# Per-chunk offsets on another engine, one gate moved, one branch begun with a gate, and rows split by two engines

## The chip, the cores and the metric

The kernel runs on one core of a Trainium2 chip. The core has five engines that work side by side, each through its own queue in order: TensorE (PE, matmuls), VectorE (DVE), ScalarE (ACT), GpSimd (POOL) and SyncE (SP, here the issuer of all DMAs). PEld in the profile is TensorE's loading of weights. The metric is the device time of one execution in microseconds; less is better.

## The reference

Two layers of a decoder, 1024 tokens of width 1024, 16 learned meta tokens in front (1040 rows), fp32. Cut to what matters:

```python
def hybrid_layer(x, ...):
    h = rmsnorm(x, norm_g)
    proj = h @ w_in                       # split into A, B, C and the gates
    log_f = log_sigmoid(a_f + b_f)        # 8 heads
    log_cum = cumsum(log_f, axis=1)
    y_a = forgetting attention(a_q, a_k, a_v, log_cum)
    cq, ckv = rmsnorm(b_cq, g_cq), rmsnorm(b_ckv, g_ckv)
    y_b = latent attention(cq @ w_uq, ckv @ w_ukv, rotary key b_kr)
    y_c = sliding-window attention with sinks(rope(c_q), rope(c_k), c_v)
    # y_n * silu(z_n) @ w_branch[n], n = 0, 1, 2, merged by sigmoid gates
    m = sum(sigmoid(gates[n]) * ((y_n * silu(z_n)) @ w_branch[n]))
    return x + m @ w_out
```

## The kernel before

All activations lie transposed: channels on the 128 partitions, rows (tokens) on the free axis, cut into chunks `FULL` (264, 264, 512 columns), `TOK` (two of 512) in layer 2 where only the tokens count, and `END` (four of 256) for the rows of the output projection. Every fp32 product is three matmuls on a high and a low part of each operand, `mm3` (L175 hh with wh, L176 hl with wh, L177 hh with wl). `split` makes the two parts: the high part is a cast on ACT (L157), the low part a subtraction (L158), on DVE for activations and on POOL for weights (`weights`, L158 `wl<-wr,wh`). Results land in PSUM banks named `ps_s`, `ps_pj`, `ps_t`, `ps_o`, two of each; a bank is used again when the engine that empties it is through.

A layer goes through these stages:

- **Side work and sliding-window projections.** `side_work` is a generator that computes the cumulative log-forget values on 8 partitions, beside the projections of C's keys and queries (`rotate`, L222 to L232, on DVE and POOL; casts of `sg`, L157, on ACT; L227 and L230 read the banks). The cumulative sum is made in nine cuts (16 and eight of 128 columns): a scan per cut (L579), the last column of each into `tot` (L581), a scan over the nine totals into `off` (L585), and the addition of each offset to its cut (L587).
- **Low rank, values, kn and wuq.** The latent rows are projected and normed (`normed`, L201 to L212, on DVE with two ACT steps), then come `values` (L454 to L461: value blocks of 256 columns, emptied by DVE L459 and ACT L461 in turn), the keys `kn` in four pairs (casts and subtractions of `sg`, L157 and L158) and the queries `wuq`. Between these, `some()` is called at ten positions, and `EARLY[l]` says how many gate projections are run at each: positions 0 to 2 lie among the values, 3 to 6 after the four kn pairs, 7 to 9 after the parts of wuq. A gate projection is two or three chunks of 24 matmuls each, emptied by ACT alone (L657, `gt`) and written to memory.
- **Fox, mla, swa.** The three attentions. Between their blocks `fill()` takes the next entry of a list, `PLAN[l]`: `g` is a gate projection, `z` the projection of a SiLU path (ACT `ez` L734, then DVE `zs` L735 empties the bank), `r` and `s` belong to the merge. The first `fill()` of each attention stands ahead of its first block.
- **Merge.** `branch(n_, d)` for n_ = 0, 2, 1 and d = 0 to 7: per chunk the gate through a tanh (ACT L951), 12 matmuls into a bank, DVE L957 (`gt<-gt,ps`) and, for n_ of 2 and 1, DVE L958 (`acc<-acc,gt`). For n_ = 1, the last, the sum is split into `m` for the output projection, in chunks `och` of 264, 264 and 512 (layer 1) or four of 256 (layer 2).
- **Output projection (wo)**, from `m`, column by column, and in layer 2 the final norm.

Tile builds the program and orders the instructions of each engine by its own simulated timeline, so the order on an engine isn't the order of the code, and an edit can move instructions that it doesn't name. All DMAs stand in SP's queue.

Of the kernel before, what the change touches and what calls it, by code (L numbers as in the profile page):

```python
# [13 lines left out]
AF = mybir.ActivationFunctionType  # L14
ALU = mybir.AluOpType
# [3 lines left out]
P = 128  # L19
# [3 lines left out]
NM = 16  # L23
# [30 lines left out]


EARLY = ((1, 0, 0, 0, 0, 0, 0, 1, 0, 0),
         (0, 0, 0, 0, 1, 0, 0, 0, 0, 0))

# [10 lines left out]
def _f(ap):  # L71
    return ap.bitcast(F32)
# [13 lines left out]
def tile_kernel(ctx: ExitStack, tc, a, out):  # L86
    nc = tc.nc
# [66 lines left out]
    def split(hi, lo, src, scale=None, eng=None):  # L154

        if scale is None:
            nc.scalar.copy(hi, src)  # L157
            (eng or nc.vector).tensor_tensor(lo, src, _f(hi), ALU.subtract)  # L158
        else:
            nc.scalar.activation(hi, src, AF.Copy, scale=scale)  # L160
            nc.vector.scalar_tensor_tensor(lo, src, scale, _f(hi), ALU.mult, ALU.subtract)

    def weights(src, n):
        raw = wp.tile([P, 1024], F32, tag="wr", name="wr", bufs=2)
        dma(raw[:, :n], src)
        wh = wp.tile([P, 1024], F32R, tag="wh", name="wh")
        wl = wp.tile([P, 1024], F32R, tag="wl", name="wl")
        split(wh[:, :n], wl[:, :n], raw[:, :n], eng=nc.gpsimd)
        return wh, wl

    def mm3(dst, wh, wl, rh, rl, nk, m, c0, c1):

        for k in range(nk):
            w1 = wh[:, k * P:k * P + m]
            nc.tensor.matmul(dst, w1, rh[:, k, c0:c1], start=(k == 0), stop=False)  # L175
            nc.tensor.matmul(dst, w1, rl[:, k, c0:c1], start=False, stop=False)  # L176
            nc.tensor.matmul(dst, wl[:, k * P:k * P + m], rh[:, k, c0:c1],  # L177
                             start=False, stop=(k == nk - 1))
# [343 lines left out]
    for l in range(DEPTH):  # L522
# [33 lines left out]
        def side_work():  # L556

            c16 = pa.tile([32, L], F32, tag="c16", name="c16", bufs=1)
            s16 = pa.tile([64, L], F32, tag="s16", name="s16", bufs=1)
            dma(c16, a["c16"][:32])  # L560
            dma(s16[32:64], a["sn16"])
            fr = pa.tile([H, L], F32, tag="fr", name="fr", bufs=1)
            x = pa.tile([H, L], F32, tag="fx", name="fx", bufs=1)
            e = pa.tile([H, L], F32, tag="fe", name="fe", bufs=1)
            nc.scalar.copy(fr, krt[64:72])
            nc.vector.tensor_scalar(x, fr, bfc[:, l:l + 1], None, ALU.add)
            nc.vector.scalar_tensor_tensor(e, x, -1.0, x, ALU.mult, ALU.min)
            nc.scalar.activation(e, e, AF.Exp)
            nc.scalar.activation(e, e, AF.Ln, bias=ones[:H, 0:1])
            yield  # L570
            nc.vector.scalar_tensor_tensor(x, x, 0.0, e, ALU.min, ALU.subtract)
            cuts = [(0, NM)] + [(NM + i * P, NM + (i + 1) * P) for i in range(NB)]
            z8 = pa.tile([H, P], F32, tag="z8", name="z8", bufs=1)
            nc.vector.memset(z8, 0.0)
            tot = pa.tile([H, 16], F32, tag="tot", name="tot", bufs=1)
            off = pa.tile([H, 16], F32, tag="off", name="off", bufs=1)
            nc.vector.memset(off, 0.0)
            for n_, (c0, c1) in enumerate(cuts):
                nc.vector.tensor_tensor_scan(e[:, c0:c1], x[:, c0:c1], z8[:, :c1 - c0], 0.0,  # L579
                                             ALU.add, ALU.add)  # L580
                nc.vector.tensor_copy(tot[:, n_:n_ + 1], e[:, c1 - 1:c1])  # L581
                if n_ == 4:
                    yield
            yield
            nc.vector.tensor_tensor_scan(off[:, 1:10], tot[:, 0:9], z8[:, :9], 0.0, ALU.add, ALU.add)  # L585
            for n_, (c0, c1) in enumerate(cuts):
                nc.vector.tensor_scalar(e[:, c0:c1], e[:, c0:c1], off[:, n_:n_ + 1], None, ALU.add)  # L587
            dma(ck_d, e)
            yield
            r1 = pa.tile([32, L], F32, tag="r1", name="r1", bufs=1)  # L590
            r2 = pa.tile([32, L], F32, tag="r2", name="r2", bufs=1)
            kr = [pa.tile([32, L], F32R, tag=f"kr{x_}", name="kr", bufs=1) for x_ in range(2)]
            nc.vector.tensor_tensor(r1, krt[0:32], c16, ALU.mult)
            nc.vector.tensor_tensor(r2, krt[32:64], s16[32:64], ALU.mult)
            yield
            nc.vector.tensor_tensor(r1, r1, r2, ALU.add)
            split(kr[0], kr[1], r1)
            for n_ in range(2):
                dma(kr_d[n_], kr[n_])
# [129 lines left out]
        def filler(br):  # L729
            plan, zs = list(PLAN[l][(0, 2, 1)[br]]), []  # L730

            def ev_z(t, c0, c1):
                e = fin.tile([P, 512], F32, tag="gt", name="ez", bufs=GT)[:, :c1 - c0]
                nc.scalar.activation(e, t, AF.Tanh, scale=0.5)  # L734
                nc.vector.scalar_tensor_tensor(zs[-1][:, c0:c1], e, 1.0, t, ALU.add, ALU.mult)  # L735

            def fill():
                for kind in plan.pop(0) if plan else "":
                    if kind == "r":
                        merge_starts()  # L740
                    elif kind == "s":
                        branch(0, merged.pop(0), "pj")
                    elif kind == "z":
                        zs.append(fin.tile([P, L], F32, tag="zs", name="zs", bufs=2))
                        proj(w1[T_Z + 4 * br + len(zs) - 1], KD, hh, hl, qch, ev_z, tag="pj")
                    elif kind == "g":
                        gate(fin, "pj")
                finish_late()
            return fill, zs
# [72 lines left out]
        with tc.tile_pool(name=f"swk{l}", bufs=2, side=A, reuse_waits="tile") as pk, \  # L822
# [12 lines left out]
            for kv in range(2):  # L835
# [14 lines left out]
                for i in range(-1 if first else 0, NB):  # L850
# [90 lines left out]
        def branch(n_, d, tag=None):  # L941

            if d % 2 == 0:
                wbr[:] = weights(a["wbr"][l, n_, d // 2], 1024)
            w = [x[:, 512 * (d % 2):512 * (d % 2) + 512] for x in wbr]
            gr = (gp2 if gp2 and d % 2 else gp).tile([P, L], F32, tag="gt", name="gt", bufs=2)
            dma(gr[:, lo:], gate_d[KD * n_ + d, :, lo:])
            for c0, c1 in qch:
                n = c1 - c0
                g = gr[:, c0:c1]  # L950
                nc.scalar.activation(g, g, AF.Tanh, scale=0.5)  # L951
                t = (psum(tag) if tag else dense())[:, :n]
                mm3(t, w[0], w[1], ys[0], ys[1], 4, P, c0, c1)
                if n_ == 0:
                    nc.vector.scalar_tensor_tensor(acc[:, d, c0:c1], g, 1.0, t, ALU.add, ALU.mult)
                else:
                    nc.vector.scalar_tensor_tensor(g, g, 1.0, t, ALU.add, ALU.mult)  # L957
                    nc.vector.tensor_tensor(acc[:, d, c0:c1], acc[:, d, c0:c1], g, ALU.add)  # L958
            if n_ == 1:
                for c0, c1 in och:  # L960
                    split(mt[c0][0][:, d], mt[c0][1][:, d], acc[:, d, c0:c1])

        with tc.tile_pool(name=f"mla{l}", bufs=2, side=B, reuse_waits="tile") as pm:
            fill, zs = filler(1)
# [68 lines left out]
        with tc.tile_pool(name=f"so{l}", bufs=2, side=B, reuse_waits="tile") as po:  # L1033
# [21 lines left out]
            for c0, c1 in och:  # L1055
# [6 lines left out]
                else:  # L1062
# [110 lines left out]
```

## Time and profile before

| | |
|---|---|
| median of 3 runs | 2587.16 us (2586.63 to 2590.52) |
| profiled execution, its own time | 2592.05 us |
| its span, first to last instruction | 2590.3 us |
| mean granted TensorE clock | 0.993 |
| TensorE busy | 98% of the span |
| DVE, ACT, POOL busy | 50%, 46%, 38% |
| DMA | 303.40 MB, mean 117 GB/s |

The page says for each engine how long it worked; since TensorE works nearly all the time, the page's averages say little about this change. What is to be read are the few places at which TensorE stands: the windows (busy time by stretch, with the granted clock), the table of waits (which instruction released the waiting one), and the rows of single instructions in order of time, in which a bracket `[idle before <-releaser]` stands behind an instruction that had to wait. In a row, `64x512` are partitions and elements per partition, and `x3` three instructions of one group drawn together.

### The profile page before, as it was taken

The numbers are of one execution on the slowest core, as the hardware profiler recorded it, in microseconds if no ns is written. First come the engines' busy times: TensorE is split into PE (matmuls) and PEld (weight loads), VectorE is DVE, ScalarE is ACT, GpSimd is POOL, SyncE is SP. The second block draws the span as 40 slices with busy tenths as digits, with TensorE's granted clock in tenths as the row PEclk, the third lists the DMA queues.
The fourth block names the chain that finished last, engine by engine and source line by source line (L and its number), as shares of the span: only waits on it lengthen the run. The fifth ranks groups of instructions, "written<-read, shape, count | busy, mean of one in ns | idle before, by whom it ended". The sixth has DMA issues, their size and how long they took to land.

```text
span 2590.3 us, 42110 instructions
## 1 busy us (share of the span) xinstructions
PE 2527.6 (98%) x15446; PEld 2256.7 (87%) x15446; DVE 1286.9 (50%) x3339; ACT 1199.9 (46%) x2684; POOL 996.0 (38%) x966
## 2 busy tenths in 40 slices
PE   8999999999999999999999999999999999999998
PEld 7989899999888999899998878888887888887887
DVE  6464355544363445657156453455434623565743
ACT  5234345545474456644232333455445634666433
POOL 2141545354332424462523325445323332353433
PEclk9999999999999999999999999999999999999999
DMA  5144512222634434364333353221226363453532
GB/s 169 55 136 136 205 54 81 73 74 79 172 104 118 124 98 127 101 225 167 112 90 87 105 197 128 74 80 60 90 71 177 101 167 84 124 140 129 173 123 74
DMA packets 137631, 303.40 MB, mean 117 GB/s; under 512 B 22560, under 2 KB 63296, under 8 KB 137424
## 3 DMA queue, kind: packets, MB, share of 16 engines
q1 hardware_dynamic: 137424, 300.71, 37.7%
q8 instruction: 122, 2.00, 0.3%
q14 instruction: 85, 0.70, 0.1%
HBM read 211.98 MB, written 88.66 MB: 116 GB/s over the span
## 4 chain that ended last, share of the span: by engine, by line
PE 77%; DMA 5%; DVE 4%; ACT 2%; issue 2%; POOL 1%; SPq 1%; POOLq 0%; ACTq 0%; DVEq 0%
PE ps_pj L175 14%; PE ps_pj L176 14%; PE ps_pj L177 14%; PE ps_t L268 5%; PE ps_s L999 3%; PE ps_o L312 3%; PE ps_o L310 2%; PE ps_s L176 2%; PE ps_s L175 2%; PE ps_s L177 2%; PE ps_s L804 1%; PE ps_s L802 1%; PE ps_o L176 1%; PE ps_o L175 1%; PE ps_o L177 1%
## 5 line engine op out<-in xcount | busy, mean ns | idle before, releaser
L158 POOL TENSOR_TENSOR wl<-wr,wh 128x1024 fp32r<-128x1024 f32 (+1 forms) x156 | 376.6, 2414 | 838.3 <-ACT wh L157 712.2
L175 PE MATMUL ps_pj<-hh,wh 128*128 128x512 f32 (+1 forms) x1920 | 674.3, 351 | 3.6 <-DVE zs L735 2.2
L176 PE MATMUL ps_pj<-hl,wh 128*128 128x512 f32 (+1 forms) x1920 | 672.7, 350 | 0.0
L177 PE MATMUL ps_pj<-hh,wl 128*128 128x512 f32 (+1 forms) x1920 | 671.3, 350 | 1.4 <-POOL wl L158 1.4
L175 PEld LDWEIGHTS ps_pj<-hh,wh 128*128 128x128 f32 x1920 | 363.2, 189 | 46.6 <-DVE zs L735 3.2
L177 PEld LDWEIGHTS ps_pj<-hh,wl 128*128 128x128 f32 x1920 | 363.4, 189 | 43.0 <-POOL wl L158 2.0
L176 PEld LDWEIGHTS ps_pj<-hl,wh 128*128 128x128 f32 x1920 | 363.1, 189 | 39.8 <-issue 0.5
L158 DVE TENSOR_TENSOR ptl<-ps_t,pth 128x512 fp32r<-128x512 f32 (+1 forms) x386 | 244.7, 641 | 140.6 <-ACT pth L157 134.3
L157 ACT CAST pth<-ps_t 128x512 fp32r<-128x512 f32 (+1 forms) x386 | 205.8, 547 | 169.0 <-PE ps_t L268 140.9
L260 ACT ACTIVATE P<-P,mn 128x656 f32<-128x656 f32 (+8 forms) x272 | 206.9, 761 | 164.7 <-DVE mn L255 160.1
L157 ACT CAST wh<-wr 128x1024 fp32r<-128x1024 f32 (+1 forms) x156 | 162.1, 1039 | 249.9 <-PE ps_pj L176 146.9
L268 PE MATMUL ps_t<-ident,P 128*128 128x128 f32 x1152 | 187.6, 276 | 0.8 <-DVE ptl L158 0.7
L310 PE MATMUL ps_o<-pth,vp 128*128 128x256 f32 (+1 forms) x640 | 168.4, 278 | 4.5 <-DVE u L281 3.1
L312 PE MATMUL ps_o<-ptl,vp 128*128 128x256 f32 (+1 forms) x640 | 160.4, 288 | 2.4 <-DVE ptl L158 2.2
L298 POOL COPY pmeta<-P 128x16 f32<-128x16 f32 x256 | 49.6, 198 | 276.2 <-ACT P L260 272.8
L999 PE MATMUL ps_s<-kt,qt 96*128 96x328 f32 (+9 forms) x696 | 146.8, 328 | 3.1 <-DVE mn L255 3.0
L268 PEld LDWEIGHTS ps_t<-ident,P 128*128 128x128 f32 x1152 | 134.9, 141 | 9.0 <-DVE ptl L158 1.5
L310 PEld LDWEIGHTS ps_o<-pth,vp 128*128 128x128 f32 x640 | 121.4, 190 | 13.2 <-issue 3.0
L809 POOL TENSOR_TENSOR cm<-ckb,tri 128x128 f32<-128x128 f32 (+1 forms) x136 | 60.4, 446 | 184.9 <-DVE mn L255 181.4
L312 PEld LDWEIGHTS ps_o<-ptl,vp 128*128 128x128 f32 x640 | 121.2, 189 | 9.2 <-DVE ptl L158 5.4
L281 DVE TENSOR_TENSOR u<-ps_o,hv 64x256 f32<-64x256 f32 x128 | 53.9, 421 | 138.0 <-ACT hv L280 121.6
L999 PEld LDWEIGHTS ps_s<-kt,qt 96*128 96x128 f32 (+1 forms) x696 | 108.5, 187 | 10.3 <-DVE mn L255 5.5
(353 smaller groups left out, 5645.8 us busy)
## 6 DMA issues: line engine op xcount, KB each, us to landing
wr<-in_w_dram SPq DMA_DIRECT2D x108, 512.0 KB
gate_d<-gt SPq DMA_DIRECT2D x72, 256.0 KB
gt<-gate_d SPq DMA_DIRECT2D x24, 520.0 KB
wr<-in_wbr_dram SPq DMA_DIRECT2D x24, 512.0 KB
gt<-gate_d SPq DMA_DIRECT2D x24, 512.0 KB
kn_d<-sg SPq DMA_DIRECT2D x16, 520.0 KB
ckb<-ck_d SPq DMA_DIRECT2D x16, 520.0 KB
kt<-kn_d SPq DMA_DIRECT2D x16, 520.0 KB
```

The lines of the kernel that those rows point to most:

```text
L157: nc.scalar.copy(hi, src)
L158: (eng or nc.vector).tensor_tensor(lo, src, _f(hi), ALU.subtract)
L175: nc.tensor.matmul(dst, w1, rh[:, k, c0:c1], start=(k == 0), stop=False)
L176: nc.tensor.matmul(dst, w1, rl[:, k, c0:c1], start=False, stop=False)
L177: nc.tensor.matmul(dst, wl[:, k * P:k * P + m], rh[:, k, c0:c1], start=False, stop=(k == nk - 1))
L260: nc.scalar.activation(s[:rows, :n], s[:rows, :n], AF.Exp, bias=prev, scale=-1.0, accum_out=total)
L268: nc.tensor.transpose(t[:kk, c:c + rows], src, ident[:rows, :rows])
L281: nc.vector.tensor_tensor(u[mine, :n], o[mine, :n], t[mine, :n], ALU.add)
L310: nc.tensor.matmul(dst, vp[:, j + x, vs], ph[:, cols], start=(j + x == 0), stop=False)
L312: nc.tensor.matmul(dst, vp[:, j + x, vs], pl[:, cols], start=False, stop=(diag and x == 1))
L809: nc.gpsimd.tensor_tensor(cm[:rows, :rows], ckb[:rows, d:n], tri[:rows, :rows], ALU.add)
L999: nc.tensor.matmul(dst, q[:, qi, q0:q0 + rows], kt[:, ki, c0:c1], start=(x == 0), stop=(x == 2))
```

## The change

Four edits:

1. In `side_work`, both layers: the nine copies into `tot` become one ACT copy of a strided column set, and the nine additions of the offsets (L587) become ACT activations of the kind Identity with the offset as bias.
2. `EARLY[1]`: layer 2's one early gate is taken from position 4 (after the second kn pair) to position 1 (among the values).
3. `PLAN[1][0]`, fox of layer 2: the first fill is a gate; the first z comes a fill later, and a later fill runs one gate fewer, so that nine gates and four z remain.
4. In `branch` with n_ = 1: the rows are split as soon as their chunk of `acc` is summed, no longer after all chunks of d, and of the pieces in `och` those with an odd number have their low part subtracted on POOL. In layer 1 this is the second of three (8 subtractions of 264 columns), in layer 2 the second and fourth of four (16 of 256).

```diff
--- before.py
+++ after.py
@@ -54,7 +54,7 @@
 
 
 EARLY = ((1, 0, 0, 0, 0, 0, 0, 1, 0, 0),
-         (0, 0, 0, 0, 1, 0, 0, 0, 0, 0))
+         (0, 1, 0, 0, 0, 0, 0, 0, 0, 0))
 
 
 
@@ -62,7 +62,7 @@
     ("z . z . . . gg g . g z g z g g . gg".split(),
      "gg zzg . . . gg zz . gg".split(),
      "g g . z g z g . g g zzr s . . sss s s".split()),
-    ("z . . . z . gg . . gg z . z g gg . gg".split(),
+    ("g z . . z . g . . gg z . z g gg . gg".split(),
      "gg zg z g . gg zz g gg".split(),
      "g gg . z . z g . . g zzr . ss . ss s s".split()),
 )
@@ -578,13 +578,13 @@
             for n_, (c0, c1) in enumerate(cuts):
                 nc.vector.tensor_tensor_scan(e[:, c0:c1], x[:, c0:c1], z8[:, :c1 - c0], 0.0,
                                              ALU.add, ALU.add)
-                nc.vector.tensor_copy(tot[:, n_:n_ + 1], e[:, c1 - 1:c1])
                 if n_ == 4:
                     yield
+            nc.scalar.copy(tot[:, :9], e[:, NM - 1::P])
             yield
             nc.vector.tensor_tensor_scan(off[:, 1:10], tot[:, 0:9], z8[:, :9], 0.0, ALU.add, ALU.add)
             for n_, (c0, c1) in enumerate(cuts):
-                nc.vector.tensor_scalar(e[:, c0:c1], e[:, c0:c1], off[:, n_:n_ + 1], None, ALU.add)
+                nc.scalar.activation(e[:, c0:c1], e[:, c0:c1], AF.Identity, bias=off[:, n_:n_ + 1])
             dma(ck_d, e)
             yield
             r1 = pa.tile([32, L], F32, tag="r1", name="r1", bufs=1)
@@ -956,9 +956,11 @@
                 else:
                     nc.vector.scalar_tensor_tensor(g, g, 1.0, t, ALU.add, ALU.mult)
                     nc.vector.tensor_tensor(acc[:, d, c0:c1], acc[:, d, c0:c1], g, ALU.add)
-            if n_ == 1:
-                for c0, c1 in och:
-                    split(mt[c0][0][:, d], mt[c0][1][:, d], acc[:, d, c0:c1])
+                if n_ == 1:
+                    for i, (m0, m1) in enumerate(och):
+                        if c0 <= m0 < c1:
+                            split(mt[m0][0][:, d], mt[m0][1][:, d], acc[:, d, m0:m1],
+                                  eng=nc.gpsimd if i % 2 else None)
 
         with tc.tile_pool(name=f"mla{l}", bufs=2, side=B, reuse_waits="tile") as pm:
             fill, zs = filler(1)
```

No matmul and no DMA is added or taken away. In layer 1 the order of TensorE's instructions is the same in both kernels; in layer 2 it differs in the values, kn, wuq and fox.

First place, DVE in layer 1's side work (`fe` are the cumulative sums, `ro` and `sg` the rotated rows of C's projections and their split). Before:

```order
L228 TENSOR_TENSOR ro_1100<-cx_1097,s_977 64x512
L227 TENSOR_TENSOR ro_1099<-ps_t,c_976 64x512
L230 TENSOR_TENSOR ro_1102<-ps_t,s_977 64x512
L585 SCALAR_TENSOR_TENSOR off<-tot,z_1278 8x9
L158 TENSOR_TENSOR sg_983<-ro_1060,sg_982 64x264
L587 TENSOR_SCALAR fe<-fe,off 8x128 x5
L229 TENSOR_TENSOR ro_1101<-cx_1097,c_976 64x512
L587 TENSOR_SCALAR fe<-fe,off 8x128 x3
L228 TENSOR_TENSOR ro_1188<-ps_s,s_977 128x264
L158 TENSOR_TENSOR sg_981<-ro_1099,sg_980 64x512
L227 TENSOR_TENSOR ro_1187<-ps_o,c_976 128x264
L230 TENSOR_TENSOR ro_1190<-ps_o,s_977 128x264
```

and after:

```order
L158 TENSOR_TENSOR sg_981<-ro_1058,sg_980 64x264
L227 TENSOR_TENSOR ro_1099<-ps_t,c_976 64x512
L228 TENSOR_TENSOR ro_1100<-cx_1097,s_977 64x512
L585 SCALAR_TENSOR_TENSOR off<-tot,z_1278 8x9
L230 TENSOR_TENSOR ro_1102<-ps_t,s_977 64x512
L158 TENSOR_TENSOR sg_983<-ro_1060,sg_982 64x264
L229 TENSOR_TENSOR ro_1101<-cx_1097,c_976 64x512
L228 TENSOR_TENSOR ro_1188<-ps_s,s_977 128x264
L158 TENSOR_TENSOR sg_981<-ro_1099,sg_980 64x512
L432 MEMSET xm 128x96
L227 TENSOR_TENSOR ro_1187<-ps_o,c_976 128x264
L230 TENSOR_TENSOR ro_1190<-ps_o,s_977 128x264
```

The additions into `fe` are gone from between the rotation's steps; the scan into `off` moved ahead of L230 of the 512-column chunk, and `ps_o` is read by L227 and L230 behind the subtraction into `sg` as before. On ACT, in the same place, the offsets now stand between the casts; after:

```order
L157 CAST sg_980<-ro_1058 64x264
L614 COPY cx_1097<-ps_t 64x512
L583 COPY tot<-fe 8x9
L587 ACTIVATE fe<-fe,off 8x16
L157 CAST sg_982<-ro_1060 64x264
L587 ACTIVATE fe<-fe,off 8x128 x8
L157 CAST sg_980<-ro_1099 64x512
L157 CAST wh<-wr 128x1024
L157 CAST sg_982<-ro_1101 64x512
```

Second place, ACT in layer 2 from the last value blocks to the kn pairs (`cqh` is the high part of the normed cq, `vst` value blocks, `gt` the early gate, `sg` kn). Before:

```order
L461 COPY vst<-ps_s 128x256 x3
L157 CAST cqh<-ps_o 128x512
L447 COPY vst<-ps_s 16x256
L447 COPY vst<-ps_pj 16x256
L157 CAST cqh<-ps_o 128x512 x3
L157 CAST sg_16853<-ps_s 128x264
L157 CAST sg_16853<-ps_pj 128x264
L157 CAST sg_16853<-ps_s 128x512
L157 CAST sg_16884<-ps_pj 128x264
L157 CAST sg_16884<-ps_s 128x264
L157 CAST sg_16884<-ps_pj 128x512
L657 COPY gt<-ps_s 128x512
```

and after:

```order
L157 CAST cqh<-ps_o 128x512
L461 COPY vst<-ps_s 128x256
L157 CAST cqh<-ps_o 128x512 x2
L657 COPY gt<-ps_s 128x512
L157 CAST cqh<-ps_o 128x512 x3
L157 CAST wh<-wr 128x768
L657 COPY gt<-ps_pj 128x512
L461 COPY vst<-ps_s 128x256 x3
L447 COPY vst<-ps_s 16x256
L447 COPY vst<-ps_pj 16x256
L157 CAST sg_16899<-ps_s 128x264
L157 CAST sg_16899<-ps_pj 128x264
```

The gate's two copies (`gt`) moved from behind the second kn pair (six casts into `sg`) to between the value blocks, ahead of the last three `vst` and of all kn pairs.

Third place, DVE at the end of n_ = 1 in layer 2 (`gt<-gt,ps` and `acc` as above, `m` the low parts). Before:

```order
L957 SCALAR_TENSOR_TENSOR gt<-gt,ps_pj 128x512
L958 TENSOR_TENSOR acc<-acc,gt 128x512
L158 TENSOR_TENSOR m_26272<-acc,m_26271 128x256
L158 TENSOR_TENSOR m_26274<-acc,m_26273 128x256
L957 SCALAR_TENSOR_TENSOR gt<-gt,ps_t 128x512
L958 TENSOR_TENSOR acc<-acc,gt 128x512
L158 TENSOR_TENSOR m_26268<-acc,m_26267 128x256
L957 SCALAR_TENSOR_TENSOR gt<-gt,ps_o 128x512
L158 TENSOR_TENSOR m_26270<-acc,m_26269 128x256
L958 TENSOR_TENSOR acc<-acc,gt 128x512
L158 TENSOR_TENSOR m_26272<-acc,m_26271 128x256
L158 TENSOR_TENSOR m_26274<-acc,m_26273 128x256
```

and after:

```order
L957 SCALAR_TENSOR_TENSOR gt<-gt,ps_s 128x512
L958 TENSOR_TENSOR acc<-acc,gt 128x512
L158 TENSOR_TENSOR m_26252<-acc,m_26251 128x256
L957 SCALAR_TENSOR_TENSOR gt<-gt,ps_pj 128x512
L958 TENSOR_TENSOR acc<-acc,gt 128x512
L158 TENSOR_TENSOR m_26256<-acc,m_26255 128x256
L957 SCALAR_TENSOR_TENSOR gt<-gt,ps_t 128x512
L958 TENSOR_TENSOR acc<-acc,gt 128x512
L158 TENSOR_TENSOR m_26252<-acc,m_26251 128x256
L957 SCALAR_TENSOR_TENSOR gt<-gt,ps_o 128x512
L958 TENSOR_TENSOR acc<-acc,gt 128x512
L158 TENSOR_TENSOR m_26256<-acc,m_26255 128x256
```

On POOL, in the same stretch, the other half of the subtractions stands between the low parts of the weights; after:

```order
L158 TENSOR_TENSOR wl<-wr,wh 128x1024
L158 TENSOR_TENSOR m_26258<-acc,m_26257 128x256
L158 TENSOR_TENSOR m_26254<-acc,m_26253 128x256
L158 TENSOR_TENSOR m_26258<-acc,m_26257 128x256
L158 TENSOR_TENSOR m_26254<-acc,m_26253 128x256
L158 TENSOR_TENSOR wl<-wr,wh 128x1024
L158 TENSOR_TENSOR m_26258<-acc,m_26257 128x256
L158 TENSOR_TENSOR wl<-wr,wh 128x1024
```

Of the two subtractions of a chunk, one is left on DVE, always behind its `acc`.

## The prediction

> **What bounds the kernel now.** I read the page's first part, then windows of the stages that the change touches, then TensorE's waits, and at each wait the rows of the engines in order of time.
>
> ```profile
> span 2590.3 us, 42110 instructions
> PE 2527.6 (98%) x15446; PEld 2256.7 (87%) x15446; DVE 1286.9 (50%) x3339; ACT 1199.9 (46%) x2684; POOL 996.0 (38%) x966
> ```
>
> TensorE (PE) is busy for 2527.6 of 2590.3 us and loses no instruction by the change. So only its 62.7 us without work, and stretches in which its clock is halved, can give time back; the other engines' busy shares don't matter by themselves. A window row gives its length, the busy time and count of PE, PEld, DVE, ACT and POOL, then the granted clock (PEclk), DMA share and GB/s:
>
> ```profile
> 120.00:140.00 20.00, 15.46 (x82) 13.87 (x81) 19.45 (x42) 6.43 (x11) 11.99 (x10) 0.83 0.35 82
> 1380.00:1400.00 20.00, 20.00 (x87) 16.16 (x86) 19.30 (x41) 7.14 (x11) 8.14 (x6) 1.00 0.18 59
> 1400.00:1420.00 20.00, 18.61 (x81) 14.77 (x80) 17.36 (x25) 6.39 (x10) 14.16 (x10) 1.00 0.42 108
> 1480.00:1500.00 20.00, 19.11 (x118) 16.25 (x116) 10.33 (x17) 8.48 (x17) 2.55 (x2) 1.00 0.30 93
> 1500.00:1520.00 20.00, 16.95 (x89) 14.16 (x88) 11.76 (x23) 6.03 (x14) 0.00 (x0) 0.91 0.57 214
> 1560.00:1580.00 20.00, 17.83 (x94) 15.56 (x93) 3.01 (x6) 3.52 (x7) 12.04 (x10) 0.91 0.67 233
> 2480.00:2500.00 20.00, 16.20 (x121) 15.96 (x121) 9.12 (x16) 6.63 (x14) 6.05 (x3) 0.91 0.59 226
> ```
>
> The row 1380 to 1400 shows PE undisturbed: 87 matmuls in 20 us, 0.23 us each. The other rows are stages of the change, with 4.54, 1.39, 0.89, 3.05, 2.17 and 3.80 us in which PE stood. A clock of 0.91 means that another 0.09 x 20 = 1.8 us of clock are lost there, and 0.83 means 3.4 us, part of it while PE stood anyway. The clock falls in the windows with waits of 2.2 us and more, and not in the one with 1.39 us. The waits and what released them (total, times, longest):
>
> ```profile
> PE ps_o L175 <- DVE ro L230: 4.5, 1, 4.5
> PE ps_s L175 <- ACT m L157: 3.7, 1, 3.7
> PE ps_s L175 <- DVE sg L158: 2.4, 1, 2.4
> PE ps_pj L175 <- DVE zs L735: 2.2, 1, 2.2
> ```
>
> **A and B: the offsets go to ScalarE.** Layer 1's side work:
>
> ```profile
> 123.29 0.94 DVE L585 TENSOR_TENSOR_SCAN off<-tot,z 8x9 f32<-8x9 f32 x1
> 124.23 0.62 ACT L157 CAST sg<-ro 64x512 fp32r<-64x512 f32 x1 [2.71 <-POOL ro L231]
> 124.49 1.06 DVE L587 TENSOR_SCALAR fe<-fe,off 8x128 f32<-8x128 f32 x5
> 126.08 4.08 DVE L587 TENSOR_SCALAR fe<-fe,off 8x128 f32<-8x128 f32 x3
> 126.29 1.28 POOL L232 TENSOR_TENSOR ro<-ro,ro 64x512 f32<-64x512 f32 x1 [2.09 <-DVE ro L229]
> 127.54 2.34 POOL L158 TENSOR_TENSOR wl<-wr,wh 128x1024 fp32r<-128x1024 f32 x1
> 131.48 0.42 DVE L230 TENSOR_TENSOR ro<-ps_o,s 128x264 f32<-128x264 f32 x1
> 131.96 0.59 PE L175 MATMUL ps_o<-hh,wh 128*128 128x264 f32 x1 [4.54 <-DVE ro L230]
> L333 ACT ACTIVATE rt<-ps_t 18x128 f32<-18x128 f32 x8 | 2.1, 265 | 8.5 <-PE ps_t L331 8.5
> ```
>
> Five additions (L587) take 1.06 us, and the last three take 4.08 us: they end only after GpSimd's (POOL's) two instructions have ended at 129.88. Behind them on VectorE (DVE) stands L230, which frees the bank that PE waits for. The change takes all nine additions and the nine copies ahead of the scan off VectorE. ScalarE (ACT) gets one copy and nine activations, ahead of its cast of sg. No row shows such an activation. The 18x128 row bounds it from above at 0.27 us; from below I take the 0.20 us between VectorE's starts (1.06 us for five). Eight cost 1.6 to 2.1 us. In the new order the scan stands before one of the three 512-column steps that it stood behind, and without the copies it starts about 1.2 us earlier and ends at 123.0; the activations end at about 125, the cast at 125.7. VectorE's subtraction behind the cast may be held by L232 until about 126.3 and ends at 127.0; L227 and L230 follow by 127.7. PE wants the bank at 131.96 - 4.54 = 127.4, so 0.3 us of wait are left, and the halved clock behind it goes. Of its 3.4 us some 1.2 fall on idle time: 2.2 count. The most is 4.5 + 2.2 = 6.7; the least 3.0, if a wait of 1.5 us stays; I take 5.5, near the upper end since the additions are gone from the queue. ScalarE's casts of weights come half a microsecond later, which costs nothing: PE has the rest of the group of two chunks to work off before it uses them.
>
> [...]
>
> B: in layer 2 the same additions stall the same way, and PE's 1.39 us in the window 1400 to 1420 lie ten microseconds behind that, for weights that GpSimd makes late. VectorE comes 3.7 us earlier to them. Bounds 0 (the weights are late anyway) and 1.4; I take 1.2.
>
> **C: the early gate among the values (layer 2).**
>
> ```profile
> 1508.06 0.73 DVE L212 SCALAR_TENSOR_TENSOR ps_o<-raw,gcol,ps_t 128x512 f32<-128x512 f32 x1
> 1510.06 0.42 DVE L158 TENSOR_TENSOR sg<-ps_s,sg 128x264 fp32r<-128x264 f32 x1
> 1510.54 0.39 PE L175 MATMUL ps_s<-cvh,wh 128*128 128x264 f32 x1 [2.38 <-DVE sg L158]
> 1527.10 0.43 DVE L158 TENSOR_TENSOR sg<-ps_s,sg 128x264 fp32r<-128x264 f32 x1 [12.18 <-ACT sg L157]
> ```
>
> VectorE is late with the norm of cq (L212) and the copies of values, so PE waits up to 2.38 us for banks; a few microseconds on, VectorE is idle for 12.18 us, since the gate that PE then works on needs only ScalarE. The gate is 48 matmuls, 48 x 0.23 = 11.0 us. It now stands after ten value blocks, so VectorE works off its arrears under it. The 0.89 us before 1500 stay, as they lie ahead of it; the 3.05 us and 1.8 us of clock behind can go: at most 4.85, at least 2 if a new wait of 2 us comes elsewhere. I take 4.3. What is late next: the kn pairs now follow each other without the gate's 11 us between, but the casts and subtractions of one pair (six of each) fit under its matmuls, as they do at 1527; and the 768-column weights, which start once the gate has left its buffer, are needed behind eighteen value matmuls.
>
> **D: the forgetting branch begins with a gate (layer 2).**
>
> ```profile
> 1567.39 1.04 ACT L157 CAST wh<-wr 128x1024 fp32r<-128x1024 f32 x1 [8.32 <-PE ps_pj L176]
> 1568.34 1.08 ACT L734 ACTIVATE ez<-ps_pj 128x512 f32<-128x512 f32 x2
> 1568.96 1.29 DVE L735 SCALAR_TENSOR_TENSOR zs<-ez,ps_pj 128x512 f32<-128x512 f32 x2 [10.47 <-ACT ez L734]
> 1569.70 0.39 PE L175 MATMUL ps_pj<-hh,wh 128*128 128x264 f32 x1 [2.17 <-DVE zs L735]
> ```
>
> ScalarE's cast of weights, its first ez and VectorE's zs stand in a chain before the bank is free. With a gate, one copy (L657) takes the place of ez and zs. The bank is free 0.65 us earlier (1569.65 less the end of the first ez at about 1569.0), and the wait becomes 1.5 us, about the length at which no halved clock was seen. Least 0.6, most 2.17 + 1.8 = 4.0; I take 2.2, as the cast stays in front. The later exchange of a z fill for a gate in that stage leaves PE's work equal; I put it at 0, within 1 either way, since no row here prices it.
>
> **E: merged rows split chunk by chunk (n = 1, layer 2).**
>
> ```profile
> 2470.03 0.68 DVE L957 SCALAR_TENSOR_TENSOR gt<-gt,ps_t 128x512 f32<-128x512 f32 x1
> 2472.47 0.68 DVE L957 SCALAR_TENSOR_TENSOR gt<-gt,ps_o 128x512 f32<-128x512 f32 x1
> 2473.43 2.92 POOL L158 TENSOR_TENSOR wl<-wr,wh 128x1024 fp32r<-128x1024 f32 x1 [7.90 <-ACT wh L157]
> 2474.56 2.07 DVE L158 TENSOR_TENSOR m<-acc,m 128x256 fp32r<-128x256 f32 x1 [0.47 <-ACT m L157]
> 2476.55 0.68 DVE L957 SCALAR_TENSOR_TENSOR gt<-gt,ps_s 128x512 f32<-128x512 f32 x1
> 2481.87 0.68 DVE L957 SCALAR_TENSOR_TENSOR gt<-gt,ps_t 128x512 f32<-128x512 f32 x1
> 2484.09 0.68 DVE L957 SCALAR_TENSOR_TENSOR gt<-gt,ps_o 128x512 f32<-128x512 f32 x1
> L958 DVE TENSOR_TENSOR acc<-acc,gt 128x512 f32<-128x512 f32 x48 | 47.0, 986 | 0.9
> L222 POOL TENSOR_TENSOR sq<-sq,sqt 128x256 f32<-128x256 f32 x24 | 17.5, 739 | 31.4 <-ACT sqt L221 31.4
> ```
>
> A chunk of this branch is 12 matmuls, 12 x 0.23 = 2.8 us. VectorE needs 2.44 us (2470.03 to 2472.47), and 4.08 where a subtraction sits under GpSimd's wl; three plain chunks and one such make 11.4 against PE's 11.1, so it never catches up and PE waits 3.7 us (the waits above) for the last rows. After: one of two subtractions per chunk is GpSimd's, and VectorE's chunk is 2.2 us, as from 2481.87 to 2484.09, which holds one of them. Over 16 chunks this gives 16 x 0.24 = 3.8 us, and where the delayed one is now GpSimd's, 1.6 more for each. GpSimd's 16 subtractions cost 0.74 each by the nearest form (L222), 3.0 in four chunks beside 2.9 of wl: it has time. The window's 3.80 + 1.8 us are the most; the least is below nothing (rivals); I take 4.3. Layer 1's same branch (1160 to 1240) has PE busy throughout, so it gives 0:
>
> ```profile
> 1160.00:1240.00 80.00, 80.00 (x511) 72.87 (x510) 53.42 (x90) 30.95 (x60) 24.94 (x13) 1.00 0.49 165
> ```
>
> [...]
>
> **Sum.** 5.5 + 1.2 + 4.3 + 2.2 + 4.3 = 17.5 us. The profiled execution took 2592.05 us, 4.9 above the median of the runs, 2587.16; less 17.5 it is 2574.5, and on the runs' scale 2569.7. I say 2570.
>
> **Rivals.**
> First: GpSimd's subtractions hold VectorE. A held one costs at most its 0.74 us, the 2.07 row shows that holding happens. If it hits one addition into acc per chunk, VectorE's chunk is 2.9 us against 2.8, no arrears are made up, E gives 0: 2574. For it: VectorE's acc step has two operands in SBUF like the held m. Against: GpSimd's step falls mostly beside gt, which reads PSUM.
> Second, on the other side: the same holding, but of both VectorE steps of a chunk (acc and m), and of GpSimd's own wl. VectorE's chunk is then 2.2 + 1.5 = 3.7 us, 0.9 over PE's; 16 x 0.9 = 14 us are added at the end of the branch, with PE at half clock for perhaps half of it (7). E is then -21, and the sum -21 + 13.2 = -8: 2595, slower. It decides when VectorE's chunk passes 3.3 us: 16 x 0.5 x 1.5 = 12 eats the rest.
> Third: ScalarE, now in the chain, is late by 2 us or more, since its activations wait for the scan and the cast for them: A gives 3, B 0, 2573.5; with D's halved clock staying as well, 2575.5.
> Fourth: the halved stretches merely move to other waits, and new waits for VectorE appear behind the kn pairs; A, C, D and E keep a third: 2581 to 2585, about no change.
>
> **How the numbers follow.** Forecast, four or five of the waits gone: 0.58. First rival 0.15, third 0.10, fourth 0.11 (half of it within 0.2%), second 0.06. 0.2% is 5.2 us, about what can be told from no change here. Faster by over 0.2%: 0.58 + 0.15 + 0.10 + 0.05 = 0.88, less 0.03 from the forecast's own tail: 0.85; within: 0.09; slower: 0.06. Range: the upper ends 6.7 + 1.4 + 4.85 + 2.4 + 5.6 = 21 give 2566, and with up to 4 more for D's cast and smaller waits 2562; at the other end the three partial rivals reach 2576, and half of the fourth 2583.
>
> **What would show it.** A: no L587 on DVE, the wait for ro L230 under 1 us, clock 1.00 in 120 to 140. B: no wait for wl near 1413. C: the 12-us idle of DVE gone, the wait for sg L158 gone. D: the wait for zs at the start of fox replaced by one of about 1.5 us for ACT's gt. E: the wait for m at the start of wo under 1 us, while the mean of L958 128x512 (986 ns in the groups above) stays. Wrong would be: a longer L958, a wait of PE for ACT sg in the side work, or halved clocks at other places.

## The result: 14 us less, and the profile after

| | before | after |
|---|---|---|
| median | 2587.63 us (6 runs, 2586.63 to 2590.52) | 2574.41 us (6 runs, 2569.85 to 2578.36) |
| ratio | | 0.9946, 95% interval 0.9933 to 0.9959 |
| profiled execution | 2592.05 us | 2569.85 us |
| span, mean granted clock | 2590.3 us, 0.993 | 2567.8 us, 0.998 |

The ratio is 14.0 us (10.6 to 17.3); the medians differ by 13.2. The two profiled executions are 22.2 us apart: the one of before took longer than its six timed runs, and the one of after is the fastest of its six. So the traces tell where time went, and the timed runs how much. Two of e1's twelve executions below took 8764 and 9988 us and are left out of its ratio. The stages of the change after it, as windows (columns as in the prediction):

```profile
120.00:140.00 20.00, 18.99 (x127) 17.28 (x126) 17.20 (x26) 9.12 (x22) 15.58 (x12) 1.00 0.50 134
1380.00:1400.00 20.00, 18.58 (x80) 14.75 (x79) 18.61 (x33) 8.68 (x20) 10.40 (x8) 1.00 0.35 87
1480.00:1500.00 20.00, 19.73 (x115) 16.91 (x115) 16.62 (x27) 9.32 (x19) 2.16 (x2) 1.00 0.49 153
1500.00:1520.00 20.00, 20.00 (x126) 17.97 (x125) 7.30 (x16) 7.33 (x17) 1.15 (x2) 1.00 0.61 227
1540.00:1560.00 20.00, 18.05 (x100) 15.10 (x99) 2.40 (x6) 6.45 (x10) 12.17 (x9) 1.00 0.98 356
2460.00:2480.00 20.00, 19.55 (x161) 19.15 (x161) 7.89 (x14) 7.49 (x16) 8.96 (x7) 1.00 0.63 246
```

TensorE stands 1.01, 1.42, 0.27, 0, 1.95 and 0.45 us there, where it stood 4.54, 1.39, 0.89, 3.05, 2.17 and 3.80, and the clock is 1.00 in all six. What is left of the waits:

```profile
PE ps_pj L175 <- ACT gt L657: 2.0, 2, 1.4
PE ps_s L177 <- POOL wl L158: 1.4, 1, 1.4
PE ps_pj L177 <- POOL wl L158: 0.9, 1, 0.9
PE ps_s L175 <- ACT m L157: 0.4, 1, 0.4
```

Layer 1's side work (prediction's A) in order of time:

```profile
121.58 2.45 ACT L587 ACTIVATE fe<-fe,off 8x128 f32<-8x128 f32 x8 [0.44 <-DVE off L585]
124.57 1.30 DVE L158 TENSOR_TENSOR sg<-ro,sg 64x512 fp32r<-64x512 f32 x1 [0.33 <-ACT sg L157]
126.26 0.42 DVE L230 TENSOR_TENSOR ro<-ps_o,s 128x264 f32<-128x264 f32 x1
125.57 2.55 POOL L158 TENSOR_TENSOR wl<-wr,wh 128x1024 fp32r<-128x1024 f32 x1 [0.24 <-ACT wh L157]
128.17 0.39 PE L177 MATMUL ps_pj<-hh,wl 128*128 128x264 f32 x1 [0.93 <-POOL wl L158]
```

L230 is through at 126.7, so the bank is no longer what PE waits for. It waits 0.93 us for the weights' low part (wl), which GpSimd starts only at 125.57. Of that, 0.24 us is GpSimd's wait for ScalarE's cast, which stands behind the eight activations (2.45 us from the first to the last); ahead of it GpSimd ran L232 from 124.05 to 125.33. In layer 2 (B) the longest wait for wl is as long as before, but it is another one. First before's, from the table of waits, then the rows of after:

```profile
PE ps_pj L177 <- POOL wl L158: 1.4, 1, 1.4
1393.04 1.04 ACT L157 CAST wh<-wr 128x1024 fp32r<-128x1024 f32 x1
1394.64 1.30 POOL L231 TENSOR_TENSOR ro<-ro,ro 128x512 f32<-128x512 f32 x1 [2.17 <-DVE ro L227]
1395.90 2.37 POOL L158 TENSOR_TENSOR wl<-wr,wh 128x1024 fp32r<-128x1024 f32 x1
1398.32 0.50 PE L177 MATMUL ps_s<-hh,wl 128*128 128x512 f32 x1 [1.42 <-POOL wl L158]
```

Before waited in `ps_pj` (at 1415). After doesn't wait there; it waits in `ps_s`, some 30 matmuls earlier in the program, where before didn't. The cast for this wl was done at 1394.08, but in GpSimd's new order wl stands behind L231 (in before it stood ahead of it), and L231 waited 2.17 us for VectorE's L227.

In the place of D, ScalarE's cast of weights still stands ahead of the copy:

```profile
1551.76 1.04 ACT L157 CAST wh<-wr 128x1024 fp32r<-128x1024 f32 x1 [7.52 <-PE ps_pj L176]
1552.71 1.07 ACT L657 COPY gt<-ps_pj 128x512 f32<-128x512 f32 x2
1553.35 0.40 PE L175 MATMUL ps_pj<-hh,wh 128*128 128x264 f32 x1 [1.39 <-ACT gt L657]
```

### The profile page after: what moved, and what is told of

Same layout as the page of the kernel before. It is cut to its first block, busy times and chain, and to the rows that moved or that the text cites. A ratio compares the mean times of both kernels' runs of the same rounds, so it can differ in the third digit from the quotient of the medians.

```text
span 2567.8 us, 42092 instructions
## 1 busy us (share of the span) xinstructions
PE 2517.1 (98%) x15446; PEld 2247.5 (88%) x15446; DVE 1273.4 (50%) x3279; ACT 1205.8 (47%) x2704; POOL 1012.9 (39%) x990
## 4 chain that ended last, share of the span: by engine, by line
PE 79%; DMA 5%; DVE 2%; ACT 2%; POOL 2%; issue 1%; SPq 0%; POOLq 0%; ACTq 0%; DVEq 0%
PE ps_pj L175 14%; PE ps_pj L176 14%; PE ps_pj L177 14%; PE ps_t L268 5%; PE ps_s L1001 3%; PE ps_o L312 3%; PE ps_o L310 2%; PE ps_s L177 2%; PE ps_s L176 2%; PE ps_s L175 2%; PE ps_s L804 1%; PE ps_s L802 1%; PE ps_o L176 1%; PE ps_o L177 1%; PE ps_o L175 1%
## 5 line engine op out<-in xcount | busy, mean ns | idle before, releaser
L176 PEld LDWEIGHTS ps_pj<-hl,wh 128*128 128x128 f32 x1920 | 361.4, 188 | 39.4 <-issue 0.5
```

## The experiments

Times are ratios to the kernel before, timed beside it on the same chip, and the same in us of 2588. The last five columns are TensorE's waits in that kernel's one trace: A and B in the two side works, C before the kn pairs, D at fox's start in layer 2, E at the start of layer 2's output projection.

| kernel | ratio (interval) | us | A | B | C | D | E |
|---|---|---|---|---|---|---|---|
| before | 1 | | 4.5 | 1.4 | 2.4 | 2.2 | 3.7 |
| after | 0.9946 (0.9933 to 0.9959) | -14.0 | 0.9 | 1.4 | 0 | 1.4 | 0.4 |
| e1 offsets alone | 0.9974 (0.9963 to 0.9986) | -6.7 | 0.9 | 1.4 | 2.4 | 2.2 | 3.4 |
| e2 early gate alone | 0.9967 (0.9954 to 0.9980) | -8.5 | 4.5 | 1.4 | 0 | 2.1 | 1.6 |
| e3 fox's plan alone | 0.9979 (0.9969 to 0.9989) | -5.4 | 4.5 | 1.4 | 2.4 | 1.4 | 2.3 |
| e4 split alone | 0.9996 (0.9987 to 1.0004) | -1.0 | 4.5 | 1.4 | 2.4 | 2.2 | 0.3 |
| e5 after again | 0.9948 (0.9931 to 0.9965) | -13.5 | 0.9 | 1.4 | 0 | 1.4 | 0 |
| e6 after without the split | 0.9962 (0.9947 to 0.9977) | -9.8 | 0.9 | 1.4 | 0 | 1.4 | 3.6 |
| e7 after, split on VectorE alone | 0.9956 (0.9943 to 0.9969) | -11.4 | 0.9 | 1.4 | 0 | 1.4 | 0 |
| e8 after, gate a position later | 0.9944 (0.9927 to 0.9960) | -14.5 | 0.9 | 1.4 | 0 | 1.4 | 0.3 |
| e9 copies of totals alone | 0.9982 (0.9970 to 0.9994) | -4.7 | 2.0 | 0.4 | 2.4 | 2.2 | 1.7 |
| e10 after, one addition on VectorE | 0.9967 (0.9955 to 0.9978) | -8.5 | 3.4 | 2.1 | 0 | 1.4 | 0.8 |
| e11 after, gate emptied by VectorE | 0.9954 (0.9942 to 0.9966) | -11.9 | 0.9 | 1.4 | 0 | 1.5, a chunk later | 2.2 |
| e12 e10 and e11 | 0.9959 (0.9947 to 0.9971) | -10.6 | 3.4 | 2.1 | 0 | 2.1, a chunk later | 0.3 |

**e1 to e4: one edit each, on the kernel before.** Their diffs are the four parts of the diff above.

> The first edit alone, both layers, on the kernel before. Theory (GpSimd's instruction stalls VectorE's additions, and VectorE then frees the bank late): in layer 1 TensorE's 4.5 us wait for ro L230 and the half clock behind it go, as in the changed kernel, so 5 us; in layer 2 no gain (the 1.4 us wait for wl stays, since ScalarE's activations delay the cast before it). Total -5 us. Rival (the additions were only late work on VectorE, and the wait moves to ScalarE's activations of 0.30 us each): the wait in layer 1 is 2.5 us or more, total -2 us or less.

Measured -6.7 us (3.6 to 9.6); A falls from 4.5 to 0.9 us and the clock of the window 120 to 140 returns from 0.83 to 1.00. The theory holds for layer 1. In layer 2 the 1.4 us is the other wait described above, so only the number came as said.

> The second edit alone: the early gate of layer 2 among the values. Theory (VectorE works off its arrears under the gate): TensorE's waits of 0.6, 0.7 and 2.4 us between the values and the kn pairs go, with one halved stretch: -6 to -7 us, VectorE's idle of 12 us shrinks to pieces under 2 us. Rival (the waits come back behind the kn pairs, which now follow each other): -2 us, with new waits of TensorE for sg.

Measured -8.5 us (5.2 to 11.9); the waits between values and kn are gone but for 0.2 us, and behind the kn pairs came only one of 0.3 us. The theory holds; the 6 to 7 us that it expected lie within the interval.

> The third edit alone: fox of layer 2 begun with a gate. Theory: the wait at its start falls from 2.2 to 1.5 us; the halved clock may or may not stay, so -0.7 to -2.5 us. Rival: the exchange of z and g in the rest of fox costs what the start gives: 0.

Measured -5.4 us (2.8 to 8.0); D falls from 2.2 to 1.4 us, as said. The time is more than the 0.7 us of wait and the 1.8 us of half clock make (in before the granted clock is 0.53, 0.50, 0.50 and 0.76 in the four microseconds from 1570 on, and 1.00 ahead of them and behind); what the rest is, the trace doesn't show. (The half clock isn't sure to be part of it; see D below.)

> The fourth edit alone: split chunk by chunk, the odd piece on GpSimd. Theory: the wait of 3.7 us for m at the start of layer 2's output projection falls under 0.5 us and no half clock follows: -4.6 us. Rival (GpSimd's subtractions hold VectorE): L958 128x512 gets longer than its 986 ns, gain under 2 us.

Measured -1.0 us (-3.4 to +1.0). The wait fell to 0.3 us, L958 didn't get longer, and yet the time hardly moved. This contradiction led to e6 and e7.

**e5 to e8: round the changed kernel.**

e6 puts this back:

```diff
-                if n_ == 1:
-                    for i, (m0, m1) in enumerate(och): ...
+            if n_ == 1:
+                for c0, c1 in och:
+                    split(mt[c0][0][:, d], mt[c0][1][:, d], acc[:, d, c0:c1])
```

e7 and e8:

```diff
-                            split(mt[m0][0][:, d], mt[m0][1][:, d], acc[:, d, m0:m1],
-                                  eng=nc.gpsimd if i % 2 else None)
+                            split(mt[m0][0][:, d], mt[m0][1][:, d], acc[:, d, m0:m1])
...
-         (0, 1, 0, 0, 0, 0, 0, 0, 0, 0))
+         (0, 0, 1, 0, 0, 0, 0, 0, 0, 0))
```

> The changed kernel once more, for the spread of single executions and for a time beside the next kernels. If the four parts add up (they measured -4.7, -8.2, -5.2 and -0.7 us by medians), it is 18.8 us faster than before; if the local gains of the trace are the measure, 17.9 us; if the first measurement was right, 13 us.

Again -13.5 us; the parts' ratios add up to 21.6, with an interval of some 6 us each way, against some 4 for the whole. Whether the parts fail to add up or only their errors do, stays open.

> The changed kernel without the fourth edit (split after all chunks, VectorE alone). Theory (the fourth edit is worth its local 4.7 us): 4 to 5 us slower than the changed kernel, with the wait of 3.7 us for m back. Rival (its gain is given back elsewhere, since alone it moved the median by 0.7 us only): within 1 us of the changed kernel though the wait is back.

> The changed kernel with the split chunk by chunk, but both pieces on VectorE. Theory (the gain comes from taking one subtraction of each chunk from VectorE): the wait at the start of the output projection is back at 2.5 to 3.7 us, VectorE's chunk is 2.4 us again. Rival (the gain comes from splitting each chunk at once, not from the second engine): the wait stays under 1 us.

> The changed kernel with the early gate one position later (three more value blocks ahead of it). Theory (the gate must come before VectorE's arrears fill the banks): one wait of 0.6 to 1 us ahead of the gate comes back, and the rest stays gone: 0.5 to 1 us slower than the changed kernel. Rival (any place between the norm and the kn pairs does the same): no wait over 0.5 us, no difference.

e6 gains 4 us less than after, with intervals that overlap, and the wait of 3.6 us is back. In e7 the wait is 0 though VectorE does all the subtractions, at its old 2.44 us a chunk. But e6 and e7 are one program: in their traces the instructions of every engine come in the same order, since Tile had already put each subtraction behind its chunk (as the order of before shows, third place of the change). So writing the split chunk by chunk changes nothing by itself. The fourth edit comes down to GpSimd's half of the subtractions, and the test of e7 against e6 is a test of chance: two executions of one program waited 3.6 and 0 us at this place. (e8: either of the two places does; only waits of 0.4 and 0.2 us come ahead of the gate.)

Column E is read by when the branch gets going. Before, then e11 (with the edit), then PE's wait in after, then e6 and e7 (ACT and DVE rows are at the branch's start):

```profile
2438.64 1.15 ACT L951 ACTIVATE gt<-gt 128x512 f32<-128x512 f32 x2 [5.40 <-DMA gt<-gate_d]
2441.59 1.91 DVE L158 TENSOR_TENSOR m<-acc,m 128x256 fp32r<-128x256 f32 x1 [4.15 <-ACT m L157]
2483.76 0.38 PE L175 MATMUL ps_s<-m,wh 128*128 128x256 f32 x1 [3.72 <-ACT m L157]
2430.35 1.91 DVE L158 TENSOR_TENSOR m<-acc,m 128x256 fp32r<-128x256 f32 x1 [3.86 <-ACT m L157]
2471.15 0.38 PE L175 MATMUL ps_s<-m,wh 128*128 128x256 f32 x1 [2.23 <-ACT m L157]
2462.76 0.38 PE L175 MATMUL ps_s<-m,wh 128*128 128x256 f32 x1 [0.37 <-ACT m L157]
2467.77 0.38 PE L175 MATMUL ps_s<-m,wh 128*128 128x256 f32 x1 [3.56 <-ACT m L157]
2427.34 0.42 DVE L158 TENSOR_TENSOR m<-acc,m 128x256 fp32r<-128x256 f32 x1 [2.50 <-ACT m L157]
2467.38 0.38 PE L175 MATMUL ps_s<-m,wh 128*128 128x256 f32 x1
```

VectorE's first subtraction waits for ScalarE's cast, which stands behind the gates' tanh and their loads (gt from memory): in before ScalarE stood idle 5.40 us for one of them. Call lead the time from the start of that subtraction to the moment at which PE wants the last rows (the PE row's start less its wait). Each column is one trace, in us:

| without GpSimd's half | before | e1 | e6 | e3 | e2 | e9 | e7 |
|---|---|---|---|---|---|---|---|
| lead | 38.5 | 38.5 | 38.8 | 39.4 | 39.6 | 39.8 | 40.0 |
| PE's wait | 3.7 | 3.4 | 3.6 | 2.3 | 1.6 | 1.7 | 0 |

| with it | e11 | e10 | after | e8 | e5 | e12 | e4 |
|---|---|---|---|---|---|---|---|
| lead | 38.6 | 39.5 | 39.6 | 39.8 | 39.8 | 40.0 | 40.4 |
| PE's wait | 2.2 | 0.8 | 0.4 | 0.3 | 0 | 0.3 | 0.3 |

At the same lead the edit saves 3.72 - 2.23 = 1.5 us (before and e11) and 1.65 - 0.37 = 1.3 us (e2 and after). The other 2 us of the 3.7 belong to the late start, which the edit doesn't touch. In e7 GpSimd's wl had ended (at 2427.13) before the first subtraction (at 2427.34), which took 0.42 us where the other traces have 1.2 to 1.9, and VectorE was through with it earlier against PE than in any other run.

The edit saves so little because VectorE's own subtraction still meets wl, which runs from 2443.28 to 2445.67 and from 2453.50 to 2456.21. The subtractions beside it take 2.42 and 2.07 us and end 0.3 us behind it; those between take 0.43 us. Rows of after:

```profile
2433.97 0.68 DVE L957 SCALAR_TENSOR_TENSOR gt<-gt,ps_s 128x512 f32<-128x512 f32 x1
2443.55 2.42 DVE L158 TENSOR_TENSOR m<-acc,m 128x256 fp32r<-128x256 f32 x1 [1.51 <-ACT m L157]
2454.42 2.07 DVE L158 TENSOR_TENSOR m<-acc,m 128x256 fp32r<-128x256 f32 x1 [0.47 <-ACT m L157]
2463.08 0.68 DVE L957 SCALAR_TENSOR_TENSOR gt<-gt,ps_o 128x512 f32<-128x512 f32 x1
```

Before has the same two at 2.43 and 2.07 us. From the fifth chunk's L957 to the last one's, VectorE takes 29.1 us here (2433.97 to 2463.08) and 30.1 in before (2454.01 to 2484.09); the other traces with the edit have 29.1 to 29.3, those without it 30.0 to 30.3, e7 among these. So 1.0 us is what the second engine gives over eleven chunks.

Why the gate's rows arrive early or late stays open.

**e9 to e12: what the additions and the casts really cost.**

e9, on the kernel before: the copies of the totals go to ScalarE, the additions stay on VectorE.

```diff
-                nc.vector.tensor_copy(tot[:, n_:n_ + 1], e[:, c1 - 1:c1])
...
+            nc.scalar.copy(tot[:, :9], e[:, NM - 1::P])
```

> The kernel before with only the nine copies of totals replaced by one on ScalarE; the nine additions stay on VectorE. All eight large additions now stand ahead of the step that starts GpSimd's next two instructions. Theory (what cost 4.5 us was that three additions met GpSimd's 1.3 and 2.3 us instructions, not the additions' own 0.2 us each): the wait for ro L230 in layer 1 falls under 1.5 us though VectorE still does the additions, as with the whole edit: -4 to -5 us. Rival (VectorE must be freed of the additions): the wait stays at 3 us or more, under -2 us.

```profile
123.87 1.64 DVE L587 TENSOR_SCALAR fe<-fe,off 8x128 f32<-8x128 f32 x8
125.26 4.01 POOL L158 TENSOR_TENSOR wl<-wr,wh 128x1024 fp32r<-128x1024 f32 x1 [1.68 <-ACT wh L157]
129.32 0.39 PE L177 MATMUL ps_pj<-hh,wl 128*128 128x264 f32 x1 [1.98 <-POOL wl L158]
130.53 0.43 DVE L230 TENSOR_TENSOR ro<-ps_o,s 128x264 f32<-128x264 f32 x1 [3.01 <-POOL ro L232]
132.11 0.29 PE L175 MATMUL ps_o<-hh,wh 128*128 128x264 f32 x1
```

The eight additions run through in 1.64 us, with GpSimd idle for nearly all of it: their place, not their length, made the 4.08 us of before. But e9 doesn't show that L230 then comes in time. L230 ends at 130.96, only 0.9 us earlier than in before (131.90), since it waits for GpSimd's L232, which now stands behind wl; and wl takes 4.01 us, where it took 2.34. That VectorE's steps beside it hold wl is likely, but not shown by itself. PE's wait for the bank is gone because Tile moved PE's matmuls into `ps_o` behind those into `ps_pj` (132.11; in before they stand ahead). What PE waits for instead is wl, 1.98 us. So 4.5 us became 2.0, between theory and rival, and by a changed order of three engines; e9 can't tell the two apart.

In layer 2 the wait for wl is 0.4 us in e9 and, in e10 below, 2.1 us. Neither has activations on ScalarE, so they are not what keeps this wait at 1.4 us in the changed kernel.

e10 and e11, on the changed kernel; e12 is both.

```diff
-            for n_, (c0, c1) in enumerate(cuts):
-                nc.scalar.activation(e[:, c0:c1], e[:, c0:c1], AF.Identity, bias=off[:, n_:n_ + 1])
+            ev_ = e[:, NM:].rearrange("p (n c) -> p n c", n=NB)
+            nc.vector.tensor_tensor(ev_, ev_, off[:, 1:9].unsqueeze(2).to_broadcast([H, NB, P]), ALU.add)
...
-                nc.scalar.copy(gt, t)
+                (nc.vector.tensor_copy if fast else nc.scalar.copy)(gt, t)      # fast: fox's first fill, layer 2
```

> The changed kernel with the nine activations replaced by one addition of 8x1024 on VectorE that repeats each offset over its 128 columns (the first offset is zero). Theory (ScalarE's activations, 2.45 us in a row, hold the cast of sg and with it the weights' low part, for which the changed kernel still waits 0.9 and 1.4 us): ScalarE is free 2.4 us earlier, the wait of 0.9 us in layer 1 and of 1.4 us in layer 2 fall under 0.5 us: -1 to -2.5 us. Rival (these waits come from GpSimd's own 1.3 and 2.4 us instructions): both stay; if the addition meets GpSimd's instruction, L230 is late again.

```profile
125.96 1.28 POOL L232 TENSOR_TENSOR ro<-ro,ro 64x512 f32<-64x512 f32 x1 [2.17 <-DVE ro L229]
127.21 2.35 POOL L158 TENSOR_TENSOR wl<-wr,wh 128x1024 fp32r<-128x1024 f32 x1
126.09 4.01 DVE L158 TENSOR_TENSOR sg<-ro,sg 64x512 fp32r<-64x512 f32 x1
130.97 0.59 PE L175 MATMUL ps_o<-hh,wh 128*128 128x264 f32 x1 [3.40 <-DVE ro L230]
```

Wrong: the gain is 5.5 us smaller than the changed kernel's (5.7 to 11.6 against 10.6 to 17.3, timed on two occasions, and the intervals overlap a little). The addition itself took 1.20 us. It stands ahead of VectorE's L229, for which GpSimd's L232 waits, so L232 starts only at 125.96. By its end the cast of weights was long done, and GpSimd's two instructions followed each other without a gap. The subtraction into sg, which stands ahead of L230, ended only after both (130.10, they at 129.56): 4.01 us, where the changed kernel takes 1.30. The stall of before is back with another instruction as its victim.

> The changed kernel with fox's first gate of layer 2 emptied by VectorE instead of ScalarE. Theory (the rest of the wait, 1.4 us, is ScalarE's cast of weights, 1.04 us, that stands ahead of its copy): the wait falls to 0.5 us, about -1 us. Rival (the bank is not what PE waits for, the weights are): it stays at 1.4 us.

```profile
1557.41 0.69 DVE L657 COPY gt<-ps_pj 128x512 f32<-128x512 f32 x1 [4.75 <-PE ps_pj L177]
1564.72 0.47 PE L175 MATMUL ps_pj<-hh,wh 128*128 128x512 f32 x1 [1.48 <-DVE ks L772]
```

The wait at fox's first bank is gone, as the theory said, and PE waits 1.48 us for a bank of the keys a chunk later. The theory was right on the bank, and there is no gain.

> The changed kernel with the single addition on VectorE and with fox's first gate emptied by VectorE. If both theories hold, 2 to 3.5 us faster than the changed kernel; if neither, the same.

The two don't help together either; its 10.6 us lie within the others. No version is faster than the changed kernel beyond the intervals.

## Why the prediction was right, and which of its sizes were off

The direction came out, and of the five waits A, C and E went and D shrank as forecast. The size is roughly right: 17.5 us forecast, 14.0 measured (10.6 to 17.3). The time alone doesn't favour the forecast: 2574.4 us is also what the first rival (2574) and the third (2573.5) gave. It is the traces that decide between them.

- **A, 5.5 us.** Idle time in the window fell from 4.54 to 1.01 us and the clock rose from 0.83 to 1.00. The bank costs PE under 0.3 us, as forecast; the 0.93 us for wl wasn't in the forecast. The part of that step on durations was off: I took 1.6 to 2.1 us for eight activations. They took 2.45 us (388 ns each, a new one each 0.30 us):

```profile
L587 ACT ACTIVATE fe<-fe,off 8x128 f32<-8x128 f32 x16 | 4.9, 388 | 0.9 <-DVE off L585 0.9
```

- **B, 1.2 us: nothing.** The wait that the prediction meant went, as it said. What it left out is that the edit changes the order of GpSimd's and PE's instructions there (PE's order differs at 1415 too, a place that the section on the change doesn't name), and that a wait of the same length comes up some 30 matmuls earlier. The third rival has the right number for B (0) by another cause: ScalarE's cast was done 0.56 us before GpSimd got to L231, and in A it cost 0.24 us.
- **C, 4.3 us.** The windows show 3.67 us of idle time and 1.8 us of clock less; alone the edit timed at 8.5 (5.2 to 11.9). Under-sized, if anything. VectorE's idle of 12.18 us among the kn pairs is gone; the longest among them is now 1.71 us. Behind them, ahead of fox, after has one new wait of 0.6 us (DVE sg L161).
- **D, 2.2 us.** The wait went from 2.17 to 1.39 us, near the 1.5 forecast. The rest of the term, 1.55 us of halved clock, is a sample: of four kernels that wait 2.1 to 2.2 us there (before, e1, e2, e4), only before's trace has a half clock behind it (0.91 in the window 1560 to 1580, where the others have 1.00). e4, with the same idle time in the same window as before (0.91):

```profile
1560.00:1580.00 20.00, 17.83 (x100) 15.31 (x99) 3.00 (x6) 4.12 (x8) 13.37 (x11) 1.00 0.55 197
```

- **E, 4.3 us: 1.3 to 1.5.** This is the mis-sized term. The step that failed is "where the delayed one is now GpSimd's, 1.6 more for each": VectorE's own subtraction beside wl is as long as before (2.42 and 2.07 us), and eleven chunks gain 1.0 us, where 0.24 us a chunk would have made 2.6. The edit alone, timed in e4, agrees with so little (1.0 us, -1.0 to 3.4). Besides, the 3.72 us of one execution is no fixed cost; some 2 us of it come and go with the arrival of the gate's rows.

With 1.4 for E and 0 for B the sum is 13.4. That this lies so near 14.0 is partly luck, since it still holds D's clock and C's 4.3, for which the edit alone timed at 8.5.

- **First and second rival:** in layer 2's branch GpSimd's subtractions don't hold VectorE. L958 128x512 has a mean of 968 ns after, 986 before, over all its uses, and the subtractions of 0.74 us run beside the step that reads PSUM (L957), which takes 0.67 or 0.68 us throughout that stretch, beside them or not. In layer 1's branch the holding does occur (L958 takes 1.20 us beside a subtraction of GpSimd's, 0.69 in most other chunks), at no cost, since PE has work throughout (80.00 of the 80 us from 1140). First layer 2, then layer 1:

```profile
2428.46 0.68 DVE L957 SCALAR_TENSOR_TENSOR gt<-gt,ps_o 128x512 f32<-128x512 f32 x1
2428.47 0.74 POOL L158 TENSOR_TENSOR m<-acc,m 128x256 fp32r<-128x256 f32 x1 [1.55 <-ACT m L157]
1176.88 1.20 DVE L958 TENSOR_TENSOR acc<-acc,gt 128x512 f32<-128x512 f32 x1
1176.77 0.76 POOL L158 TENSOR_TENSOR m<-acc,m 128x264 fp32r<-128x264 f32 x1 [2.44 <-ACT m L157]
```

So neither rival explains the time, though the holding that the first one speaks of exists. VectorE's subtraction took 4.01 us in e10 beside GpSimd's two instructions (1.30 in after), and in e9 wl took 4.01 us beside VectorE's steps (2.34 in before), which may be the same the other way round. What decides which engine is held, no run shows.

## What to carry to other kernels

Beside another engine's instructions the place of an instruction was worth more than its length here: additions of 0.2 us cost 4.5 us of wait by standing in the wrong place, and one addition in their stead cost 3.4 by the same stall. Before a wait is entered in a sum at its length, it pays to ask what sets the start of the chain that ends in it: a wait that hangs on a transfer is a sample, and one program had 3.6 and 0 us of it. Where a tool orders the instructions, the orders of two programs are worth comparing before a result is read: an edit moved work that it doesn't name (B, e9), a wait of the old length was another wait (B), and two texts were one program (e6 and e7).

## What the runs showed of the hardware

Whether a wait of TensorE is followed by a stretch of half clock differs between executions. D's wait of 2.1 to 2.2 us had one in one trace of four (above). The changed kernel, profiled twice (2569.85 and 2579.24 us), in the same stage, first after, then e5:

```profile
1040.00:1060.00 20.00, 18.50 (x135) 16.88 (x134) 15.87 (x45) 15.66 (x38) 17.83 (x23) 1.00 0.20 75
1040.00:1060.00 20.00, 18.78 (x127) 17.11 (x126) 15.26 (x45) 15.08 (x36) 15.66 (x23) 0.91 0.27 87
```

With nearly the same idle time (1.50 and 1.22 us) the stage has a clock of 1.00 in one and 0.91 in the other. In before, microsecond by microsecond, the granted clock is 0.50 from 2485 to 2488, with 0.92 and 0.88 in the two beside them: 1.7 us of clock. The waits of 2.38 us (1512 to 1516) and of 2.17 us (1570 to 1574) are followed by 1.7 us less each, and the one of 4.54 us has 3.4 us less (129 to 137), from within the wait on. So a wait's half clock can be entered in a sum only as a chance.
